# One shared product for levels 32 and 64 of a chunkwise gated recurrence, and shorter weight loads for levels 2 to 16

## Chip, cores and metric

The kernel runs on one core of one Trainium2 chip. The metric is device time in microseconds (us) of one execution. The five engines are named as in the profile: PE (TensorE: matmuls, with its weight loads shown apart as PEld), DVE (VectorE), ACT (ScalarE), POOL (GpSimd) and SP (SyncE, which issues the DMAs).

## The reference

A decoder trunk of two layers over 256 tokens and 1024 features, in float32: layer 0 is an HGRN2 gated linear recurrence, layer 1 a block-sparse attention; each is followed by a SwiGLU network, with RMS norms in between. The change touches the recurrence alone. Per head (8 heads, 128 state features, 128 value features):

```python
q = silu(q);  f = lb + (1 - lb) * sigmoid(fz);  k = 1 - f
S_t = diag(f_t) S_{t-1} + (1 - f_t) i_t^T
o_t = S_t^T q_t
```

Written without the state, `o_t` is the sum over `s <= t` of `score(t, s) * i_s`, where `score(t, s)` is the inner product, over the 128 features, of `q_t`, `k_s` and the product of all gates `f` from `s + 1` to `t`.

## The kernel before, in words

All weights are streamed once from DRAM in the order of their use, 1024 columns at a time ("sub"). Each sub is split into a high part `whi` (a copy on ACT, L412) and a low part `wlo` (a subtraction on DVE, L414), and each activation tile is split likewise, so that a float32 product is made of three fast products (`hi*hi`, `lo*hi`, `hi*lo`). `NSUB = 6` subs are held at a time. PE's main stream is these products: 128 x 128 weights with 256 tokens as the moving operand. `mm` at L455 issues every matmul, so all rows of PE carry that line and are told apart by their tiles.

The order of the work is planned when the program is built. The class `Order` keeps a clock for each engine and a list of waiting operations, each with an estimated cost (`ct`, `ca`, `cv` for PE, ACT and DVE) and a due time. The main products advance PE's clock; between them `pump` emits what is due and ready, and an operation of PE is emitted only once its inputs have been ready for 1500 ns of the plan (`EARLY`). Every engine then executes its own list strictly in order, with semaphores.

The recurrence of one head (class `Core`) runs beside the main products of the next one. After the projections of a head, `K[1]` holds the keys and `Q[1]` the queries, 128 features on the partitions and 256 tokens along the free axis (two chunks `a` of 128 tokens). `step(m)` makes level `2m` from level `m`: in each pair of neighbouring blocks of `m` places, the queries of the second block are multiplied by the gates of the first block's total, the keys of the first block by those of the second (DVE, L785 and L787), and the other halves are copied (ACT, L789 and L792). For `m = 64` the function `last` makes `q128` and `k128`, which join the two chunks (ACT, L800 to L803).

`scores` then multiplies, for each level m, the keys `K[m]` (as weights, 128 columns per chunk) with those queries that stand in the second block of a pair (64 columns per chunk, as the moving operand): function `level`, two matmuls per level. PE runs each of these plain float32 matmuls as two pairs of a weight load and a product. Level 1 has its own, wider product with `mov` (192 columns). Levels 2 and 4 share a PSUM bank, levels 8 and 16 another, and levels 32 and 64 a third (`b3`), which also takes the 128 x 128 product of `k128` and `q128`. Masked copies on DVE (`take`, L816) carry the entries of levels 1 to 16 that belong to the causal triangle into the score matrix `pm`; for the third bank the function `far` does it with four ACT copies of whole blocks (L853 to L856). `values` multiplies `pm` with the input tile `ii`, and `result` (L874 to L878) makes the output-gated, split tile `xh`, `xl` that the output projection `hgrn_w_out` reads. That projection takes heads 0 to 5 first, and heads 6 and 7 in its last 48 main products.

Of the kernel before, what the change touches and what calls it, by code (L numbers as in the profile page):

```python
# [12 lines left out]
AF = mybir.ActivationFunctionType  # L13
OP = mybir.AluOpType

P = 128
# [266 lines left out]
def cv(n, fast=False):  # L283
    return ((n / 2 if fast else n) + 66) / 0.96


def ca(n, ptr=0):
    return n / 1.2 + 93 + 93 * ptr
# [6 lines left out]
def ct(n):  # L295
    return 4 * max(n, P) / 2.4 + 3
# [6 lines left out]
def hybrid_trunk(ctx: ExitStack, tc: tile.TileContext, wts, xT, par, gfin, tab, onehot, masks, out):  # L303
    nc = tc.nc
    V, A, G, T = nc.vector, nc.scalar, nc.gpsimd, nc.tensor
# [5 lines left out]
    od = Order()  # L311
# [7 lines left out]
    def new(tag, shape, bufs=1, dt=FT, held=False):  # L319
        return ring(tag, shape, bufs, dt).new(held)  # L320
# [37 lines left out]
    def bank(g, held=False):  # L358
        return rings["ps" + g].new(held)
# [94 lines left out]
    def mm(o, a, b, start=False, stop=False):  # L454
        T.matmul(o, a, b, start=start, stop=stop, skip_group_check=True)  # L455
# [65 lines left out]
    for k0, k1 in [(k, k + 1) for k in range(4)] + [(4, 6), (6, 8)]:  # L521
        od.op("S", 60, lambda k0=k0, k1=k1: nc.sync.dma_start(hT[:, k0:k1, :], xT[:, k0:k1, :]),  # L522
              writes=hb[k0:k1], nbytes=131072 * (k1 - k0), due=8 * k0 - 6)
# [148 lines left out]
    for i in range(2):  # L672
        od.op("V", 80, lambda i=i: V.tensor_tensor(le[:, i], gain(5 + i), lbm.tile, op=OP.subtract), reads=[lbm],
              writes=[le], due=12)
# [5 lines left out]
          writes=[oml], due=30)  # L680
# [43 lines left out]
    class Core:  # L724
# [53 lines left out]
        def step(self, m, due):  # L778
            Q, K, tot = self.Q, self.K, self.tot[m]
            nb = S // (2 * m)  # L780
            if m < 64:
                q, qn, k, kn = Q[m], Q[2 * m], K[m], K[2 * m]
                v4 = lambda t: t.tile.rearrange("p (b z m) -> p b z m", z=2, m=m)
                bc = lambda z: tot.tile.rearrange("p (b z) -> p b z", z=2)[:, :, z:z + 1].to_broadcast([P, nb, m])
                od.op("V", cv(P), lambda: V.tensor_tensor(v4(qn)[:, :, 1], v4(q)[:, :, 1], bc(0), op=OP.mult),  # L785
                      reads=[q, tot], alloc=[qn], due=due)
                od.op("V", cv(P), lambda: V.tensor_tensor(v4(kn)[:, :, 0], v4(k)[:, :, 0], bc(1), op=OP.mult),  # L787
                      reads=[k, tot], alloc=[kn], due=due)
                o = od.op("A", ca(P), lambda: A.activation(v4(qn)[:, :, 0], v4(q)[:, :, 0], AF.Copy), reads=[q],  # L789
                          writes=[qn], due=due + .1)  # L790
                o.deps.append(qn.writers[0])
                o = od.op("A", ca(P), lambda: A.activation(v4(kn)[:, :, 1], v4(k)[:, :, 1], AF.Copy), reads=[k],  # L792
                          writes=[kn], due=due + .1)
                o.deps.append(kn.writers[0])
                return
            self.q128, self.k128 = q, k = new("q128", [P, P], 2), new("k128", [P, P], 2)
            Q, K = Q[64], K[64]

            def last():
                A.activation(q[:, 64:], Q[:, 192:], AF.Copy, scale=tot[:, 2:3])  # L800
                A.activation(q[:, :64], Q[:, P:192], AF.Copy)
                A.activation(k[:, :64], K[:, :64], AF.Copy, scale=tot[:, 1:2])
                A.activation(k[:, 64:], K[:, 64:P], AF.Copy)  # L803
            od.op("A", 4 * ca(64) + 186, last, reads=[Q, K, tot], alloc=[q, k], due=due)

        def scores(self, due):
            h, Q, K, mov = self.h, self.Q, self.K, self.mov
            pm = pms[h % 2]
            moff = {m: 2 * P + P * i for i, m in enumerate(LEVELS)}

            def take(b, c, m, stride=64):
                dst = pm.tile.rearrange("p a (b z m) -> p a b z m", z=2, m=m)
                src = b[:, c:c + 2 * stride].rearrange("p (a x) -> p a x", a=2)[:, :, stride - 64:]
                src = src.rearrange("p a (b m) -> p a b m", m=m)
                msk = mk[:, moff[m]:moff[m] + P].rearrange("p (a b m) -> p a b m", a=2, m=m)
                V.copy_predicated(dst[:, 0:3:2, :, 1], msk, src)  # L816

            def level(b, c, m):
                o = Q[m].tile.rearrange("p (a b z m) -> p a b z m", a=2, z=2, m=m)[:, :, :, 1]
                for a in range(2):  # L820
                    mm(b[:, c + 64 * a:c + 64 * a + 64], K[m][:, a * P:a * P + P], o[:, a], start=(c + a == 0), stop=True)

            b0 = bank("A")

            def s0():
                for a in range(2):
                    mm(b0[:, 192 * a:192 * a + 192], K[1][:, a * P:a * P + P], mov[:, a], start=(a == 0), stop=True)
            od.op("T", 2 * ct(192), s0, reads=[K[1], mov], alloc=[b0], due=due)

            def s0e():  # L830
                v = b0[:, :384].rearrange("p (a x) -> p a x", a=2)
                V.copy_predicated(pm[:, 0:3:2, :], mk[:, :2 * P].rearrange("p (a x) -> p a x", a=2), v[:, :, :P])
            od.op("V", cv(S), s0e, reads=[b0, mk], writes=[pm], due=due)
            od.op("V", cv(P), lambda: take(b0, 0, 1, 192), reads=[b0, mk], writes=[pm], due=due)
            for m in (2, 8):
                b = bank("A")
                o1 = od.op("T", 2 * ct(64), lambda b=b, m=m: level(b, 0, m), reads=[K[m], Q[m]], alloc=[b], due=due)
                o2 = od.op("T", 2 * ct(64), lambda b=b, m=m: level(b, P, 2 * m), reads=[K[2 * m], Q[2 * m]], writes=[b],
                           due=due)
                o2.deps.append(o1)  # L840
                for i in range(2):
                    od.op("V", cv(P), lambda b=b, m=m, i=i: take(b, P * i, m << i), reads=[b, mk], writes=[pm], due=due)
            b3 = bank("A")
            o1 = od.op("T", 2 * ct(64), lambda: level(b3, 0, 32), reads=[K[32], Q[32]], alloc=[b3], due=due)
            o2 = od.op("T", 2 * ct(64), lambda: level(b3, P, 64), reads=[K[64], Q[64]], writes=[b3], due=due)
            o3 = od.op("T", ct(P), lambda: mm(b3[:, 2 * P:3 * P], self.k128.tile, self.q128.tile, stop=True),
                       reads=[self.k128, self.q128], writes=[b3], due=due)
            o2.deps.append(o1)
            o3.deps.append(o2)

            def far():
                v = b3[:, :].rearrange("p (l a x) -> p l a x", l=4, a=2)
                A.activation(pm[0:32, 0:3:2, 32:64], v[0:32, 0, :, 0:32], AF.Copy)  # L853
                A.activation(pm[64:96, 0:3:2, 96:128], v[64:96, 0, :, 32:64], AF.Copy)
                A.activation(pm[0:64, 0:3:2, 64:128], v[0:64, 1], AF.Copy)
                A.activation(pm[:, 1, :], b3[:, 2 * P:3 * P], AF.Copy)  # L856
            od.op("A", 520, far, reads=[b3], writes=[pm], due=due)

            b4 = bank("A")
            hs = slice(h * P, h * P + P)  # L860

            def values():
                mm(b4[:, :S], ii[:, 0, hs], pm[:, 0:2, :].rearrange("p a t -> p (a t)"), start=True)
                mm(b4[:, P:S], ii[:, 1, hs], pm[:, 2, :], stop=True)
            od.op("T", ct(S) + ct(P), values, reads=[ii, pm], alloc=[b4], due=due)
            self.b4 = b4
# [14 lines left out]
    for h in range(NH):  # L881
        c = Core(h)
# [21 lines left out]
    for k in range(KT):  # L904
# [13 lines left out]
          reads=[tb], alloc=[tbr], due=80)  # L918
# [3 lines left out]
    for a in range(P // REP):  # L922
# [3 lines left out]
            reads=[scr_b], writes=[bt], nbytes=131072, due=90)  # L926
# [105 lines left out]
    def attend(h, qb, kb):  # L1032
# [20 lines left out]
        def scores():  # L1053
            mm(b[:, :P], q[:, :P], k[:, :P], start=True, stop=True)
            mm(b[:, P:384], qs[:, :P], kh.tile)
            mm(b[:, P:384], qs[:, P:], kh.tile)
            mm(b[:, P:384], qs[:, :P], kl.tile, stop=True)
        od.op("T", ct(P) + 3 * MM, scores, reads=[q, k, qs, kh, kl], alloc=[b], due=8)

        def logits():  # L1060
# [50 lines left out]
    for k in range(KT):  # L1111
# [8 lines left out]
          writes=[gf], due=100)  # L1120
# [152 lines left out]
```

## Time and profile before

| | us |
|---|---|
| median of 3 runs | 634.39 |
| the three runs | 634.28, 634.39, 639.41 |
| the profiled execution, own time | 636.15 |
| span of the profiled execution | 634.3 |
| PE busy in the span | 624.0 (98%) |
| ACT busy | 360.3 (57%) |
| DVE busy | 441.2 (70%) |

The span reaches from the first to the last instruction of the profiled execution; its own time is 1.85 us longer. The recurrence of the eight heads lies between 42 and 142 us of the span. Matmuls are pipelined, so the durations of neighbouring rows of PE overlap; what one costs is read from the distance between starts. The operations that one query of the timeline merges into a row carry their count (x8).

### The profile page before, as it was taken

Reading aid. Unit: us, or ns where it says so; the run is one execution under the profiler, and the core shown is the slowest. Engines: PE = TensorE matmul, PEld = TensorE weight load, DVE = VectorE, ACT = ScalarE, POOL = GpSimd, SP = SyncE. Lnnn points to the kernel's source line nnn. Section 1 sums busy time; section 2 is a strip of 40 time slices with the busy share of each in tenths; the row PEclk is TensorE's granted clock in tenths of the full one; section 3 lists DMA queues with packets and bytes.
Section 4 is the critical chain, followed back from the end, with each engine's and each line's share of the span. In section 5 each row is a group of like instructions: output and inputs, shape, how many; then the busy total and the mean of one; then the engine's idle time right before and its main releaser. Section 6 shows DMA issues by size and latency. Waiting matters only on the chain.

```text
span 634.3 us, 12520 instructions
## 1 busy us (share of the span) xinstructions
PE 624.0 (98%) x4900; PEld 600.9 (95%) x4900; DVE 441.2 (70%) x795; ACT 360.3 (57%) x691; POOL 38.8 (6%) x74
## 2 busy tenths in 40 slices
PE   8999999999999999999999999999999999999995
PEld 6899999999999999999998899999999999999994
DVE  6998787866786666666669578876685666666653
ACT  6798877755554444444446566655574444444442
POOL 0141112100400000000000000000100000000003
PEclk9999999999999999999999999999899999999998
DMA  8973434343796666665663664545556656666501
GB/s 284 329 230 130 137 100 140 129 137 131 204 256 193 197 196 195 198 194 189 190 197 118 215 207 159 167 135 198 167 165 199 198 188 187 183 184 184 175 1 67
DMA packets 32135, 111.83 MB, mean 176 GB/s; under 512 B 3835, under 2 KB 4508, under 8 KB 32076
## 3 DMA queue, kind: packets, MB, share of 16 engines
q1 hardware_dynamic: 31052, 108.71, 53.7%
q0 software_dynamic: 448, 1.25, 1.1%
q10 hardware_dynamic: 576, 1.08, 0.5%
q8 instruction: 38, 0.62, 0.4%
q14 instruction: 21, 0.17, 0.1%
HBM read 109.78 MB, written 1.25 MB: 175 GB/s over the span
## 4 chain that ended last, share of the span: by engine, by line
PE 95%; DMA 2%; ACT 1%; DVE 1%; SPq 0%; issue 0%; ACTq 0%
PE psA L455 47%; PE psB L455 47%; DMA raw<-in_w_dram 1%; DMA bt<-in_final_dram 1%; PE psB L1080 0%; ACT whi L412 0%; PE psB L1128 0%; SPq L401 0%; DVE sqacc L559 0%; SPq L522 0%; DVE wlo L414 0%; PE psA L596 0%; ACT xh L539 0%; DVE raw L1159 0%; ACT sq L1162 0%
## 5 line engine op out<-in xcount | busy, mean ns | idle before, releaser
L414 DVE TENSOR_TENSOR wlo<-raw,whi 128x1024 fp32r<-128x1024 f32 (+1 forms) x206 | 247.8, 1213 | 112.8 <-ACT whi L412 112.6
L412 ACT ACTIVATE whi<-raw 128x1024 fp32r<-128x1024 f32 (+1 forms) x205 | 213.1, 1050 | 153.2 <-issue 66.2
L455 PE MATMUL psB<-xh,whi 128*128 128x256 f32 x608 | 173.1, 288 | 0.0
L455 PE MATMUL psB<-xh,wlo 128*128 128x256 f32 x608 | 168.6, 280 | 0.0
L455 PE MATMUL psB<-xl,whi 128*128 128x256 f32 x608 | 163.0, 279 | 0.0
L455 PE MATMUL psA<-xh,whi 128*128 128x256 f32 x544 | 150.5, 280 | 0.0
L455 PE MATMUL psA<-xh,wlo 128*128 128x256 f32 x544 | 148.8, 277 | 0.0
L455 PE MATMUL psA<-xl,whi 128*128 128x256 f32 x544 | 143.7, 277 | 0.0
L455 PEld LDWEIGHTS psB<-xh,wlo 128*128 128x128 f32 x608 | 115.4, 190 | 0.7
L455 PEld LDWEIGHTS psB<-xh,whi 128*128 128x128 f32 x608 | 115.1, 189 | 0.8
L455 PEld LDWEIGHTS psB<-xl,whi 128*128 128x128 f32 x608 | 112.4, 190 | 0.0
L455 PEld LDWEIGHTS psA<-xh,whi 128*128 128x128 f32 x544 | 102.4, 188 | 0.6 <-issue 0.5
L455 PEld LDWEIGHTS psA<-xh,wlo 128*128 128x128 f32 x544 | 102.2, 188 | 0.0
L455 PEld LDWEIGHTS psA<-xl,whi 128*128 128x128 f32 x544 | 99.2, 188 | 0.0
L455 PE MATMUL psB<-hl,whi 128*128 128x256 f32 x176 | 48.7, 277 | 0.0
L455 PE MATMUL psB<-hh,whi 128*128 128x256 f32 x176 | 48.7, 277 | 0.0
L455 PE MATMUL psB<-hh,wlo 128*128 128x256 f32 x176 | 48.7, 277 | 0.0
L939 ACT ACTIVATE u<-sgq 128x256 f32<-128x256 f32 x44 | 18.0, 410 | 39.0 <-DVE sgq L937 38.7
L455 PE MATMUL psA<-wlo,hh 128*128 128x512 f32 x88 | 34.6, 393 | 0.0
L455 PE MATMUL psA<-whi,hl 128*128 128x512 f32 x88 | 34.5, 392 | 0.0
L455 PE MATMUL psA<-whi,hh 128*128 128x512 f32 x88 | 34.5, 392 | 0.0
L455 PEld LDWEIGHTS psB<-hl,whi 128*128 128x128 f32 x176 | 33.1, 188 | 0.0
(174 smaller groups left out, 795.5 us busy)
## 6 DMA issues: line engine op xcount, KB each, us to landing
raw<-in_w_dram SPq DMA_DIRECT2D x202, 512.0 KB, 4.2
raw<-in_w_dram SPq DMA_DIRECT2D x4, 256.0 KB, 4.1
bt<-scr POOLq DMA_DIRECT2D x8, 128.0 KB, 8.2
hT<-in_x_dram SPq DMA_DIRECT2D x4, 128.0 KB, 4.8
hT<-in_x_dram SPq DMA_DIRECT2D x2, 256.0 KB, 6.9
bt<-in_final_dram ACTq DMA_DIRECT2D x1, 512.0 KB, 5.1
out_dram<-raw ACTq DMA_DIRECT2D x2, 256.0 KB, 2.3
out_dram<-raw SPq DMA_DIRECT2D x2, 256.0 KB, 2.0
```

The source lines that it names most:

```text
L412: od.op("A", ca(n), lambda h=h, r=r, o=o, n=n: A.activation(h[:, :n], r[:, o:o + n], AF.Copy), reads=[r], alloc=[h], due=due)
L414: od.op("V", cv(n), lambda h=h, lo=lo, r=r, o=o, n=n: V.tensor_tensor(lo[:, :n], r[:, o:o + n], h[:, :n].bitcast(FT), op=OP.subtract), rea ...
L455: T.matmul(o, a, b, start=start, stop=stop, skip_group_check=True)
L939: od.op("A", ca(S), lambda: A.activation(sg.tile, gs.tile, AF.Sigmoid), reads=[gs], alloc=[sg], due=due)
```

## The change

In the last step before level 64 (`m == 32`), two ACT copies are added. The first writes places 96 to 127 of each chunk of `K[32]`, which hold keys that level 32 doesn't use, with the first 32 keys of level 64. The second writes the first blocks of `Q[32]` (places 0 to 31 and 64 to 95 of each chunk), which level 32 doesn't use either, with the 64 queries of level 64. One product per chunk over all 128 columns of `K[32]` and `Q[32]` then holds the scores of both levels, so the products of `K[64]` with `Q[64]` are gone. `far` picks the blocks out of the shared product with five ACT copies in place of four. For levels 2 to 16 only the first `128 - m` keys are loaded as weights, `take` reads `128 - m` partitions, and every product in these banks starts a fresh sum.

```diff
--- before.py
+++ after.py
@@ -792,6 +792,16 @@
                 o = od.op("A", ca(P), lambda: A.activation(v4(kn)[:, :, 1], v4(k)[:, :, 1], AF.Copy), reads=[k],
                           writes=[kn], due=due + .1)
                 o.deps.append(kn.writers[0])
+                if m == 32:
+
+
+                    v2 = lambda t: t.tile.rearrange("p (a x) -> p a x", a=2)
+                    od.op("A", ca(64), lambda: A.activation(v2(k)[:, :, 96:128], v2(kn)[:, :, 0:32], AF.Copy), reads=[kn],
+                          writes=[k], due=due + .2)
+                    od.op("A", ca(P), lambda: A.activation(
+                        q.tile.rearrange("p (a y z x) -> p a y z x", a=2, y=2, z=2)[:, :, :, 0],
+                        v2(qn)[:, :, 64:128].rearrange("p a (y x) -> p a y x", y=2), AF.Copy), reads=[qn], writes=[q],
+                        due=due + .2)
                 return
             self.q128, self.k128 = q, k = new("q128", [P, P], 2), new("k128", [P, P], 2)
             Q, K = Q[64], K[64]
@@ -813,12 +823,14 @@
                 src = b[:, c:c + 2 * stride].rearrange("p (a x) -> p a x", a=2)[:, :, stride - 64:]
                 src = src.rearrange("p a (b m) -> p a b m", m=m)
                 msk = mk[:, moff[m]:moff[m] + P].rearrange("p (a b m) -> p a b m", a=2, m=m)
-                V.copy_predicated(dst[:, 0:3:2, :, 1], msk, src)
+                r = P - m
+                V.copy_predicated(dst[:r, 0:3:2, :, 1], msk[:r], src[:r])
 
             def level(b, c, m):
+
                 o = Q[m].tile.rearrange("p (a b z m) -> p a b z m", a=2, z=2, m=m)[:, :, :, 1]
                 for a in range(2):
-                    mm(b[:, c + 64 * a:c + 64 * a + 64], K[m][:, a * P:a * P + P], o[:, a], start=(c + a == 0), stop=True)
+                    mm(b[:P - m, c + 64 * a:c + 64 * a + 64], K[m][:, a * P:a * P + P - m], o[:, a], start=True, stop=True)
 
             b0 = bank("A")
 
@@ -841,20 +853,26 @@
                 for i in range(2):
                     od.op("V", cv(P), lambda b=b, m=m, i=i: take(b, P * i, m << i), reads=[b, mk], writes=[pm], due=due)
             b3 = bank("A")
-            o1 = od.op("T", 2 * ct(64), lambda: level(b3, 0, 32), reads=[K[32], Q[32]], alloc=[b3], due=due)
-            o2 = od.op("T", 2 * ct(64), lambda: level(b3, P, 64), reads=[K[64], Q[64]], writes=[b3], due=due)
-            o3 = od.op("T", ct(P), lambda: mm(b3[:, 2 * P:3 * P], self.k128.tile, self.q128.tile, stop=True),
+
+            def both():
+                for a in range(2):
+                    c = slice(a * P, a * P + P)
+                    mm(b3[:, c], K[32][:, c], Q[32][:, c], start=True, stop=True)
+            o2 = od.op("T", 2 * ct(P), both, reads=[K[32], Q[32]], alloc=[b3], due=due)
+            o3 = od.op("T", ct(P), lambda: mm(b3[:, 2 * P:3 * P], self.k128.tile, self.q128.tile, start=True, stop=True),
                        reads=[self.k128, self.q128], writes=[b3], due=due)
-            o2.deps.append(o1)
             o3.deps.append(o2)
 
             def far():
-                v = b3[:, :].rearrange("p (l a x) -> p l a x", l=4, a=2)
-                A.activation(pm[0:32, 0:3:2, 32:64], v[0:32, 0, :, 0:32], AF.Copy)
-                A.activation(pm[64:96, 0:3:2, 96:128], v[64:96, 0, :, 32:64], AF.Copy)
-                A.activation(pm[0:64, 0:3:2, 64:128], v[0:64, 1], AF.Copy)
+                v = b3[:, :2 * P].rearrange("p (a x) -> p a x", a=2)
+                w = b3[:, :2 * P].rearrange("p (a y z x) -> p a y z x", a=2, y=2, z=2)[:, :, :, 0]
+                to = pm[:, 0:3:2, 64:128].rearrange("p a (y x) -> p a y x", y=2)
+                A.activation(pm[0:32, 0:3:2, 32:64], v[0:32, :, 32:64], AF.Copy)
+                A.activation(pm[64:96, 0:3:2, 96:128], v[64:96, :, 96:128], AF.Copy)
+                A.activation(to[32:64], w[32:64], AF.Copy)
+                A.activation(to[0:32], w[96:128], AF.Copy)
                 A.activation(pm[:, 1, :], b3[:, 2 * P:3 * P], AF.Copy)
-            od.op("A", 520, far, reads=[b3], writes=[pm], due=due)
+            od.op("A", 680, far, reads=[b3], writes=[pm], due=due)
 
             b4 = bank("A")
             hs = slice(h * P, h * P + P)
```

## Rows read from the trace of the kernel before

**Rows 1.** The page: busy us, share of the span, instructions of each engine.
```profile
PE 624.0 (98%) x4900; PEld 600.9 (95%) x4900; DVE 441.2 (70%) x795; ACT 360.3 (57%) x691; POOL 38.8 (6%) x74
```

**Rows 2.** The page: the chain that ended last, by engine.
```profile
PE 95%; DMA 2%; ACT 1%; DVE 1%; SPq 0%; issue 0%; ACTq 0%
```

**Rows 3.** Busy time in windows: stretch, length, engines, clock, DMA share, GB/s.
```profile
core 0: us, PE busy (x) PEld busy (x) DVE busy (x) ACT busy (x) POOL busy (x), PEclk, DMA share, GB/s
42.00:138.00 96.00, 96.00 (x810) 95.64 (x809) 76.87 (x197) 73.63 (x235) 17.39 (x42) 1.00 0.41 132
```

**Rows 4.** Timeline around 54 us: start us, us, engine, line, operation, out<-in.
```profile
54.13 0.98 PEld L455 LDWEIGHTS psA<-q,k 128*128 128x128 f32 x8
54.24 1.00 PE L455 MATMUL psA<-q,k 128*128 128x64 f32 x8
...
55.02 0.19 PEld L455 LDWEIGHTS psB<-xh,whi 128*128 128x128 f32 x1
55.05 0.36 PE L455 MATMUL psB<-xh,whi 128*128 128x256 f32 x1
...
55.25 0.28 PE L455 MATMUL psB<-xh,wlo 128*128 128x256 f32 x1
```

**Rows 5.** Timeline of PE around 62 us: the product of k128 and q128.
```profile
61.73 0.38 PE L455 MATMUL psA<-q,k 128*128 128x128 f32 x2
61.87 0.36 PE L455 MATMUL psB<-xh,whi 128*128 128x256 f32 x1
62.07 0.28 PE L455 MATMUL psB<-xh,wlo 128*128 128x256 f32 x1
```

**Rows 6.** Groups of PE by form: count | busy us, mean ns | idle before.
```profile
L455 PE MATMUL psA<-q,k 128*128 128x64 f32 x192 | 25.2, 264 | 0.0
```

**Rows 7.** Groups of ACT over the span: count | busy us, mean ns | idle before.
```profile
L789 ACT ACTIVATE q<-q 128x128 f32<-128x128 f32 x48 | 14.7, 306 | 1.3 <-DVE q L785 1.2
...
L855 ACT ACTIVATE pm<-psA 64x128 f32<-64x128 f32 x8 | 2.2, 272 | 0.1
...
L803 ACT ACTIVATE k<-k 128x64 f32<-128x64 f32 x8 | 1.9, 242 | 0.0
```

**Rows 8.** Timeline of ACT around 54 us: copies one behind the other.
```profile
54.36 0.26 ACT L856 ACTIVATE pm<-psA 128x128 f32<-128x128 f32 x1
54.52 0.30 ACT L789 ACTIVATE q<-q 128x128 f32<-128x128 f32 x1
54.72 0.30 ACT L792 ACTIVATE k<-k 128x128 f32<-128x128 f32 x1
```

**Rows 9.** Waits, 42 to 142 us: who waited for whom: us, times, longest.
```profile
ACT whi L412 <- PE psB L455: 2.7, 2, 1.9
```

**Rows 10.** The last head: timeline of DVE, then products by tile (first to last start).
```profile
142.42 0.42 DVE L878 TENSOR_TENSOR xl<-u,xh 128x256 fp32r<-128x256 f32 x1
...
L455 PE MATMUL psA<-xh,whi x14: 281/281/384, 154.8 to 159.7; 128*128 128x256 f32 x14
```

**Rows 11.** Timeline at 159 us: weights that fill 33 rows of the array.
```profile
158.88 0.29 PEld L455 LDWEIGHTS psB<-oh,tbr 33*128 33x128 f32 x2
158.88 0.91 PE L455 MATMUL psB<-oh,tbr 33*128 33x384 f32 x2
...
159.72 0.19 PEld L455 LDWEIGHTS psA<-xh,whi 128*128 128x128 f32 x1 [0.55 <-issue]
```

**Rows 12.** The chain in order of time: start us, us, what, products.
```profile
168.47 16.73 PE psA L455 x142
...
196.25 5.44 PE psA L455 x48
...
532.10 5.65 PE psB L455 x48
```

**Rows 13.** Timeline of PE at 447 us, then busy time in the window behind it.
```profile
447.10 1.02 PE L455 MATMUL psA<-ones,sqacc 128*128 128x1 f32 x8 [0.97 <-DVE sqacc L559]
...
449.00:453.00 4.00, 4.00 (x24) 4.00 (x23) 1.70 (x3) 0.76 (x3) 1.60 (x1) 0.57 0.81 233
```

## Prediction

> **What bounds the kernel now.** I read the page's shares first, then the chain, then windows over the stretch that the change touches. PE is busy for 98% of the span, DVE and ACT for 70% and 57% [rows 1]; the chain that ended last is PE for 95% [rows 2]. A share says nothing yet of this stage, so the window counts: from 42 to 138 us, where the recurrence of the heads runs beside the main products, PE is busy for 96.00 of 96.00 us, ACT for 73.63 and DVE for 76.87, at full granted clock [rows 3]. PE waits for nobody there. What leaves PE's list in this stretch comes off the end, unless another engine falls behind.
>
> What does a product of the recurrence cost PE? Its duration (264 ns) is no answer, since neighbours overlap; the distance between starts is. Eight products of 64 columns start at 54.24, the main product behind them at 55.05 and the next at 55.25 [rows 4]: 1.01 us for eight small products and one main one. A main product takes 0.118 us (142 of them in 16.73 us) [rows 12], so eight take 0.89 us, 0.112 each. Their loads say the same: eight from 54.13 to 55.02, 0.111 each. Now the product with 128 columns: two instructions and one main product from 61.73 to 62.07 [rows 5], 0.34 - 0.118 = 0.222, again 0.111 each. Twice the moving columns at the same price: in these products the weight load of 128 columns sets the pace, and the moving operand rides along.
>
> **The change, part by part.**
>
> *Levels 32 and 64 on PE.* There are 192 instructions of 64 columns [rows 6], which is 8 heads x 6 levels x 2 chunks x 2 passes. Levels 32 and 64 are 8 of them per head. In their place stand 2 chunks x 2 passes = 4 of 128 columns. By the two distances above, 8 x 0.112 = 0.89 us becomes 4 x 0.111 = 0.445 us: 0.446 us per head, 3.6 us over eight. No row has four of 128 columns in a line; were each to take as long as a main product (0.118), the saving would be 3.4 us. I take 3.6.
>
> *Shorter loads.* Levels 2, 4, 8 and 16 make 4 loads each per head, and leave out 2, 4, 8 and 16 of 128 columns. If a load's time goes with its columns, this is 4 x 0.112 x 30/128 = 0.105 us per head, 0.84 us in all; if a load costs 0.112 whatever it holds, nothing. Every load of the trace with all rows in use has 128 columns, so no row decides. I take 0.8: since the moving columns don't matter, the load is what is timed, and it is the load that shrinks; both ends stay in the range. Beside this stands the Trainium skill, "TensorE: Matmul & The Clock Gate", section "LDWEIGHTS (loading the stationary operand)": the time of a load is its number of columns divided by 1.2 GHz. By it this part would be an estimated 8 x 4 x 30/1.2 ns = 0.8 us and the whole 4.4 us; no run here shows a shorter load.
>
> *Fresh sums* (start on every product) change no count of instructions: nothing. *Masked copies* on 126 to 112 partitions have as many elements per partition as before: nothing, and DVE has 19 us to spare [rows 3].
>
> *ACT.* Added per head: a copy of 128x64 (as L803, 242 ns), one of 128x128 (as L789, 306 ns), and a fifth copy in `far`, where a 64x128 copy (272 ns) becomes two of 32x128 that I price alike [rows 7]. That is 0.82 us per head by duration, 6.6 us in all; by distance between starts, 0.16 and 0.20 us [rows 8], about 0.54 per head and 4.3 in all. ACT goes from 73.63 of 96 us to 78 to 80 of some 92: 85 to 87%. I cost it at nothing, because PE is hidden from ACT by the weights made in advance. ACT twice waits for PE to give a weight buffer back before it can make the next `whi` [rows 9]; then all six subs are full, and they are worth 6 x 8 x 3 products x 0.118 = 17 us of PE. Even 6.6 us of extra ACT work eats less than half. If that cover were gone, each microsecond of ACT would be one of PE, and the gain would turn into a loss of 2.2 us.
>
> *Waits.* The level-32 product used to need step 16 alone; the shared one needs step 32 and both fills, some 0.4 us of ACT behind it. On PE the next head's main products queue behind it, and the plan issues it 1.5 us after its inputs are due. I put that at nothing. `far` ends about 0.2 us later, and `values` and `result` behind it. For seven heads nobody on PE asks for that soon. For the last one, `xl` is done at 142.84 us [rows 10]. The first product of the next stage starts at 154.8 [rows 10], and heads 6 and 7 are read in the 48 products before it, so from 154.8 - 48 x 0.118 = 149.1 us. Of those 6.3 us the longer chain takes about 1 us, and a faster PE about another.
>
> *Sum.* 3.6 + 0.8 = 4.4 us. The profiled execution took 636.15 us, so it would take 631.75. The median of the runs is 634.39, 1.76 below the profiled one; taken from there, 630.0 us, a gain of 0.7%.
>
> **Rivals.**
>
> *1. The cadence of the main products moves.* This has nothing to do with the columns saved. The same main product comes every 0.118 us from 168 us on (16.73/142), every 0.113 from 196 on (5.44/48), and every 0.118 again from 532 on (5.65/48) [rows 12], with no change of loop at either turn. So PE has two cadences and stays in one until something disturbs it. Other groups of small products may leave it in the other. If the stretch from 188 to 338 us ran at 0.118 as well, it would cost 150 x (0.118/0.1133 - 1) = 6 us, and the kernel would end near 636. If the recurrence and its tail to 188 us, which are mostly slow now, became fast, it would gain up to 140 x 0.04 = 5 us at the very most; about 2 is nearer, since the fast cadence already shows up between groups. Then 628 or less. Likewise the granted clock averages 0.57 in the four microseconds from 449 us, mostly its lower level of 1.2 GHz, after PE had stood idle for 0.97 us and then run eight products of one column [rows 13]; that costs up to 4 x 0.43 = 1.7 us, which may come or go. Against a turn for the worse: the program behind 188 us is unchanged.
>
> *2. Short loads lose their overlap, and the kernel is slower.* Place: the 128 loads per run of levels 2 to 16. The one group with an array not full (33 rows) has no overlap: two products of 384 columns take from 158.88 to 159.72, and PEld stood idle for 0.55 us before its next load [rows 11]. At the pace of the 64-column products' own time (half of 0.112 each) behind a bare load, each of the 128 would take 0.056 us more, 7.2 us; at a full bare load each, 0.112, 14.3. With the 3.6 saved: 638 to 645. It decides as soon as a short load costs more than 3.6/128 = 0.028 us extra. Against it: that group lacks rows, not columns. The Trainium skill, "TensorEngine Tiling (Array Packing)", section "Key Properties", says that a change of tiling mode drains the engine; by its list of modes 112 columns and more are still the full-width mode, so by that rule this rival would not occur, while rows 11, with a smaller row mode, agree with a drain.
>
> *3. ACT takes the gain.* The fills make the shared product or `values` late, and PE waits at each head: 0.5 us a head is 4 us, and the kernel ends at 634. For it: ACT at 87% and strictly in order. Against it: rows 9 and the 1.5 us of the plan.
>
> *4. The load's length doesn't count.* Then 3.6 alone: 630.8.
>
> **How the numbers follow.** Forecast, with rival 4 in its reach: 0.6, 629 to 632. Rival 1, faster (626 to 628.5): 0.14; rival 1, slower (634 to 640): 0.09. Rival 2 (638 to 645): 0.07. Rival 3 (633 to 635): 0.10. The range runs from 626.5 to 636.0; it leaves out rival 2, half of slow rival 1 and a little at the low end, together under 0.2. About 1% is what a measurement tells from no change, so faster means below 628.05 and slower above 640.7. Of the fast side some 0.12 lies below 628.05, of rivals 1 and 2 some 0.05 above 640.7. The rest is 0.83.
>
> **What would show it.** In the profile after: 96 products of 128x64 gone (128 of them left, at 126 to 112 weights), 48 of 128x128 in place of 16, wait-free PE from 42 to 142 us, and a recurrence that ends some 4 us sooner. Groups of levels 2 to 16 shorter than 0.89 us per eight would show the loads right. Wrong would be: idle time of PE before `psA<-q,k` or `psA<-pm,ii` (rival 3), groups longer than 0.9 us (rival 2), or an unchanged program behind 190 us whose length has moved (rival 1).

## The result, and the profile after

The changed kernel takes 632.36 us (median of 18 runs, 631.48 to 633.65); the kernel before, run 18 times in all, 636.02 (634.28 to 639.41). The ratio is 0.9944, interval 0.9935 to 0.9953: 3.6 us faster, between 3.0 and 4.1. That is inside the range, and less than 1%, as forecast; the gain was forecast at 4.4 us. The profiled execution took 633.35 us, with a span of 631.6.

Shares and chain of the page hardly move. These two lines of the changed kernel answer to [rows 1, 2].

```profile
PE 621.1 (98%) x4868; PEld 597.7 (95%) x4868; DVE 440.2 (70%) x795; ACT 364.7 (58%) x715; POOL 36.4 (6%) x74
...
PE 94%; ACT 2%; DMA 2%; DVE 1%; issue 0%; SPq 0%; ACTq 0%
```

PE has 32 instructions less (4868 for 4900), four per head. ACT has 24 more, three per head, and its share of the chain is 2% where it was 1%. The window of the recurrence, to be held against [rows 3], shows both engines:

```profile
42.00:138.00 96.00, 95.52 (x807) 94.67 (x805) 76.39 (x195) 79.34 (x259) 14.94 (x42) 1.00 0.43 138
```

ACT is busy for 79.34 us where it was 73.63, as worked out (78 to 80). And PE is busy for 95.52 of 96.00: it waits now, which it didn't before. The waits of the changed kernel between 42 and 142 us (who waited for whom, us, times, longest) name the place; in the kernel before, no row of this list had PE in front.

```profile
PEld psA L455 <- ACT pm L874: 0.8, 1, 0.8
...
PE psA L455 <- ACT pm L874: 0.5, 1, 0.5
```

It is one wait, at one head. The timeline of the changed kernel around it:

```profile
119.78 0.61 PE L455 MATMUL psA<-q,k 128*128 128x128 f32 x4
...
120.25 1.99 ACT L412 ACTIVATE whi<-raw 128x1024 fp32r<-128x1024 f32 x2
...
121.99 0.38 PE L455 MATMUL psA<-q,k 128*128 128x128 f32 x2
...
122.62 0.92 PE L455 MATMUL psA<-mov,k 128*128 128x192 f32 x4
122.69 0.20 ACT L870 ACTIVATE pm<-psA 32x64 f32<-32x64 f32 x1
...
123.69 0.28 ACT L874 ACTIVATE pm<-psA 128x128 f32<-128x128 f32 x1
...
124.01 0.73 PEld L455 LDWEIGHTS psA<-pm,ii 128*128 128x128 f32 x4 [0.77 <-ACT pm L874]
...
124.77 0.55 PE L455 MATMUL psA<-q,k 128*126 128x64 f32 x4
```

Read it from the last row but one up. The weight loads of the product with the input tile stand idle for 0.77 us until L874, the last of the five copies of `far`, is through. The five take from 122.69 to 123.97, 1.28 us, where the plan counts 0.68; and they began 0.7 us after the start of the product of `q128` and `k128` at 121.99, because ACT had two `whi` conversions and two more copies in front of them.

What the wait costs is read from starts, against a head without it:

```profile
100.17 0.81 PE L455 MATMUL psA<-mov,k 128*128 128x192 f32 x4
100.81 0.82 PE L455 MATMUL psA<-pm,ii 128*128 128x256 f32 x4
...
101.59 0.28 PE L455 MATMUL psB<-xh,wlo 128*128 128x256 f32 x1
```

Here four products with `mov`, four with the input tile and one main product take 1.42 us, so the eight take 1.42 - 0.118 = 1.30. Around the wait the same eight take from 122.62 to 124.77, 2.15 us: 0.85 us more, within rounding the 0.84 that I use below.

The groups of small products show the two gains. First the group of level 16 (four products, 112 columns loaded), then the shared product (compare [rows 4, 5]); in each, the third row is the second main product behind the group, and 0.118 us of the distance to it belong to the first:

```profile
48.01 0.51 PE L455 MATMUL psA<-q,k 128*112 128x64 f32 x4
48.33 0.36 PE L455 MATMUL psB<-xh,whi 128*128 128x256 f32 x1
48.53 0.28 PE L455 MATMUL psB<-xh,wlo 128*128 128x256 f32 x1
...
50.18 0.61 PE L455 MATMUL psA<-q,k 128*128 128x128 f32 x4
50.55 0.36 PE L455 MATMUL psB<-xh,whi 128*128 128x256 f32 x1
50.75 0.28 PE L455 MATMUL psB<-xh,wlo 128*128 128x256 f32 x1
```

Four shared products and a main one take 0.57 us: (0.57 - 0.118)/4 = 0.113 each, the price forecast. Four of level 16 take (0.52 - 0.118)/4 = 0.1005 each, 0.011 less than with a full load.

Where does the rest of the run go? In the chain of the changed kernel (start, us, what), two pieces:

```profile
164.80 16.73 PE psA L455 x142
...
448.79 17.11 PE psB L455 x142
```

The first is the piece of [rows 12] that stood at 168.47, with the same length. The recurrence begins with the first product with `mov`, before and after at:

```profile
41.87 0.81 PE L455 MATMUL psA<-mov,k 128*128 128x192 f32 x4
```

```profile
41.53 0.81 PE L455 MATMUL psA<-mov,k 128*128 128x192 f32 x4
```

So from there to the piece it is 123.27 us where it was 126.60: 3.33 us gained. I use this length for all runs below. The second piece is 142 main products behind the last norm but one; in the chain of the kernel before, it was shorter:

```profile
452.21 16.46 PE psB L455 x142
```

Here 0.65 us is given back, in a part of the program that the change doesn't touch.

### The profile page after: what moved, and what is told of

Its sections match the earlier page's. It is cut to its first block, busy times and chain, and to the rows that moved or that the text cites. A ratio compares the mean times of both kernels' runs of the same rounds, so it can differ in the third digit from the quotient of the medians.

```text
span 631.6 us, 12483 instructions
## 1 busy us (share of the span) xinstructions
PE 621.1 (98%) x4868; PEld 597.7 (95%) x4868; DVE 440.2 (70%) x795; ACT 364.7 (58%) x715; POOL 36.4 (6%) x74
## 4 chain that ended last, share of the span: by engine, by line
PE 94%; ACT 2%; DMA 2%; DVE 1%; issue 0%; SPq 0%; ACTq 0%
PE psB L455 47%; PE psA L455 47%; DMA bt<-in_final_dram 1%; DMA raw<-in_w_dram 1%; ACT whi L412 1%; PE psB L1098 0%; PE psB L1146 0%; DVE sqacc L559 0%; PE psA L596 0%; ACT xh L539 0%; ACT k L792 0%; DVE raw L1177 0%; ACT sq L1180 0%; ACT raw L1207 0%; DVE wlo L414 0%
```

## The experiments

All are timed against the kernel before on the same chip. "Length" is that of the recurrence as above. My theory: the gain is the sum of products (3.6 us) and loads (0.64 us, from the groups of the profile after), less one wait of 0.84 us, which comes from ACT's order at one head. Rivals: ACT holds PE back throughout; shorter loads are hidden, or lose their overlap; the cadence of the main products (the distance between the starts of two neighbours) decides.

| kernel | ratio to before | interval | length, us |
|---|---|---|---|
| before | 1 | | 126.60 |
| the change | 0.9944 | 0.9935 to 0.9953 | 123.27 |
| the change again | 0.9943 | 0.9929 to 0.9957 | 123.28 |
| shared product only | 0.9952 | 0.9940 to 0.9964 | 124.17 |
| short loads only | 0.9996 | 0.9987 to 1.0005 | 126.04 |
| product issued later | 0.9930 | 0.9917 to 0.9942 | 122.47 |
| copies planned at their price | 0.9931 | 0.9916 to 0.9945 | 122.38 |
| fills on POOL | 0.9939 | 0.9923 to 0.9955 | 122.39 |
| fills on POOL, product later | 0.9933 | 0.9918 to 0.9947 | 122.24 |
| fills twice | 0.9947 | 0.9931 to 0.9964 | 123.10 |
| 96 keys loaded | 0.9920 | 0.9906 to 0.9935 | 121.93 |
| 72 keys loaded | 0.9896 | 0.9879 to 0.9913 | 120.12 |
| 64 keys loaded | 0.9996 | 0.9983 to 1.0009 | 126.08 |

### The two parts apart

The shared product alone has full loads again:

```diff
-                r = P - m
+                r = P
...
-                    mm(b[:P - m, c + 64 * a:c + 64 * a + 64], K[m][:, a * P:a * P + P - m], o[:, a], start=True, stop=True)
+                    mm(b[:, c + 64 * a:c + 64 * a + 64], K[m][:, a * P:a * P + P], o[:, a], start=True, stop=True)
```

> The changed kernel with all 128 keys loaded again at levels 2 to 16; the order of the instructions on PE is that of the changed kernel. If the parts add up (my theory): the four-product groups of levels 4, 8 and 16 go back from 0.55, 0.54 and 0.52 us (with the main product behind them) to 0.565, the run loses 8 x 0.08 = 0.64 us against the changed kernel and stays some 3 us under the kernel before (ratio 0.995). If the shorter loads are hidden (rival: the length of a load doesn't count in the end): the same time as the changed kernel, ratio 0.9944. The wait of PE near 124 us should stay in both.

Measured: ratio 0.9952, and a length of 124.17 us, 0.90 more than the change. Its group of level 16, in the timeline of PE:

```profile
48.23 0.55 PE L455 MATMUL psA<-q,k 128*128 128x64 f32 x4
...
48.79 0.28 PE L455 MATMUL psB<-xh,wlo 128*128 128x256 f32 x1
```

0.56 us in place of 0.52, at otherwise the same order of PE. The wait near 124 us is there too. So the loads are not hidden. The ratio alone could not tell 0.9952 from 0.9944, since the intervals overlap; the groups and the length can.

The length moved by 0.90 and not 0.64, and the starts of PE say why. Between two neighbouring main products it is either 0.113 or 0.118 us. In the recurrence of the change I count 238 of the one and 431 of the other, here 164 and 505: 74 x 0.0045 = 0.3 us that has nothing to do with the loads. The distances at the small products add up to 0.6.

The loads alone, in the kernel before (levels 32 and 64 keep full loads):

```diff
+                r = P - m
-                V.copy_predicated(dst[:, 0:3:2, :, 1], msk, src)
+                V.copy_predicated(dst[:r, 0:3:2, :, 1], msk[:r], src[:r])
...
+                    r = P - m if m < 32 else P
-                    mm(b[:, c + 64 * a:c + 64 * a + 64], K[m][:, a * P:a * P + P], o[:, a], start=(c + a == 0), stop=True)
+                    mm(b[:r, c + 64 * a:c + 64 * a + 64], K[m][:, a * P:a * P + r], o[:, a], start=True, stop=True)
...
```

> The kernel before with the shorter loads of levels 2 to 16 alone; levels 32 and 64 keep their own products. If the parts add up: 0.64 us faster than before, ratio 0.999, within reach of the cadence of the main products (up to 1 us either way). If the shorter loads cost their overlap somewhere (rival): slower than before. No wait of PE for ACT, since nothing is added on ACT.

Measured: 0.9996, which can't be told from no change, and a length of 126.04 us, 0.56 less than before: the size expected, and no wait of PE. The rival of slower loads falls at these widths, by the length; the ratio doesn't tell.

### The wait near 124 us

One number of the plan, the lead of the product with the input tile:

```diff
-            od.op("T", ct(S) + ct(P), values, reads=[ii, pm], alloc=[b4], due=due)
+            od.op("T", ct(S) + ct(P), values, reads=[ii, pm], alloc=[b4], due=due, early=2500.0)
```

> The changed kernel with one number of the plan changed: the product of the scores with the inputs is issued on PE 2.5 us after its scores are due, not 1.5. If the changed kernel loses 0.84 us at one place, because five ACT copies take 1.28 us where the plan has 0.68 (my theory): the wait of PE near 124 us goes, and the run is 0.8 us faster than the changed kernel, ratio 0.993. If ACT holds PE back throughout (rival): the wait moves to another head, and the time stays.

Measured: 0.9930, a length of 122.47, 0.80 less than the change. PE is busy throughout again, with ACT at least as busy as in the change:

```profile
42.00:138.00 96.00, 96.00 (x812) 95.58 (x812) 77.55 (x198) 80.11 (x265) 17.78 (x42) 1.00 0.40 136
```

No wait has PE in front, at this head or another. The next run leaves the lead alone and gives the plan the real price of the five copies:

```diff
-            od.op("A", 680, far, reads=[b3], writes=[pm], due=due)
+            od.op("A", 1280, far, reads=[b3], writes=[pm], due=due)
```

> The changed kernel with the plan's cost of the five copies of the shared product set to 1280 ns, which is what they took at the late place, in place of 680. If the wait near 124 us comes from the plan's price being 0.6 us too low (my theory): the wait goes, and the time is that of the kernel whose products of the scores are issued later, ratio 0.993. If it comes from the order of ACT at that head whatever the price (rival): a wait of 0.2 to 0.8 us remains, ratio 0.994.

Measured: 0.9931, 122.38 us, and no wait of PE:

```profile
42.00:138.00 96.00, 96.00 (x813) 95.58 (x812) 78.22 (x199) 80.15 (x262) 14.70 (x42) 1.00 0.43 139
```

Either number of the plan removes the wait; both runs reorder the other engines too, so what is shown is that a plan with more room for `far` has no wait, and that ACT's amount of work doesn't force one.

The fills on POOL take that work off ACT:

```diff
-                    od.op("A", ca(64), lambda: A.activation(v2(k)[:, :, 96:128], v2(kn)[:, :, 0:32], AF.Copy), reads=[kn],
+                    od.op("G", cg(64), lambda: G.tensor_copy(v2(k)[:, :, 96:128], v2(kn)[:, :, 0:32]), reads=[kn],
...
-                    od.op("A", ca(P), lambda: A.activation(
+                    od.op("G", cg(P), lambda: G.tensor_copy(
...
```

> The changed kernel with both fills done by POOL in place of ACT. ACT gets back 8 x 0.55 = 4.4 us of busy time, POOL has 15 us busy of 96. If ACT's load costs only the one wait of 0.84 us (my theory): 0 to 0.8 us faster than the changed kernel. If ACT holds PE back throughout (rival): faster by 2 us or more. If POOL's copies are slow (the multiplications of 128 elements on it take 0.9 us) and lengthen the chain behind the shared product: a new wait of PE, and up to 1 us slower.

Measured: 0.9939 and 122.39 us. The window:

```profile
42.00:138.00 96.00, 96.00 (x812) 95.58 (x812) 78.29 (x199) 77.58 (x246) 23.33 (x58) 1.00 0.40 139
```

ACT falls from 79.34 to 77.58 only, and PE's wait is gone; the gain in length is 0.88, that of the wait and no more. The rival asked for 2 us or more.

> Both mendings together: the fills on POOL, and the products of the scores issued 2.5 us after their inputs are due. Either alone showed no wait of PE any more. If that wait was all that ACT cost (my theory): nothing is added to either, ratio 0.993, within 0.0012. If ACT's load still costs something that shows up in no wait of PE (rival): 0.992 or less.

Both mendings together (the diffs are those above): 0.9933 and 122.24 us. Nothing is added. The opposite test gives ACT more:

```diff
+                    for _ in range(2):
...
```

(the two fills stand in the loop)

> The changed kernel with both fills done twice over, the second time without effect on the result. ACT gets 4.4 us more to do beside the recurrence. If ACT's work is hidden by weights made 12 to 19 us ahead (my theory): the time of the changed kernel, but for single waits of some tenths where five copies come late, 1 us at the most. If ACT is what takes the gain (rival): 4 us slower than the changed kernel, and no faster than before.

Measured: 0.9947 and 123.10 us, with ACT at 82.15 us of 96 in the same window and a single wait of PE's loads of 0.7 us:

```profile
42.00:138.00 96.00, 95.62 (x808) 94.87 (x807) 76.59 (x197) 82.15 (x277) 15.70 (x42) 1.00 0.41 139
```

Three amounts of ACT work, 77.6, 79.3 and 82.2 us, and the length follows none of them; it follows the one wait. The rival falls.

### How far a load can shrink

The same edit with 96, 72 and 64 in place of `P - m`. These kernels leave out the other keys of levels 2 to 16, so they measure what a load costs and are no replacement. Here 96:

```diff
-                r = P - m
+                r = 96
...
-                    mm(b[:P - m, c + 64 * a:c + 64 * a + 64], K[m][:, a * P:a * P + P - m], o[:, a], start=True, stop=True)
+                    mm(b[:96, c + 64 * a:c + 64 * a + 64], K[m][:, a * P:a * P + 96], o[:, a], start=True, stop=True)
```

> The changed kernel with 96 keys loaded at each of the levels 2 to 16; keys 96 to 127 of each chunk are left out of these levels. Order of PE as in the changed kernel. If a load shrinks by the 0.66 ns per column that levels 8 and 16 show (my theory): 32 columns less are 0.021 us, a product comes every 0.091 us, and the run is 128 x 0.021 - 0.64 = 2 us faster than the changed kernel. If it goes with its whole 0.112 us (0.875 ns per column): every 0.084 us, 2.9 us faster. If a load that isn't full loses its overlap (rival 2): slower.

The timeline of PE, a group of four and the second main product behind it:

```profile
47.76 0.47 PE L455 MATMUL psA<-q,k 128*96 128x64 f32 x4
...
48.25 0.28 PE L455 MATMUL psB<-xh,wlo 128*128 128x256 f32 x1
```

(0.49 - 0.118)/4 = 0.093 us a product, as expected from 0.66 ns per column. In length only 1.34 us is gained of 2: PE is now early enough to meet two more short waits (0.2 us each, for copies of ACT at L789 and L766), and 492 of its distances between main products are 0.118 us where the change has 431, 0.3 us more.

> The changed kernel with 64 keys loaded at each of the levels 2 to 16; keys 64 to 127 of each chunk are left out of these levels. If the time of a load goes on shrinking by 0.66 ns per column: a product every 0.070 us, 128 x 0.042 - 0.64 = 4.7 us faster than the changed kernel; 64 moving columns alone take 0.055. If a load of half the array's width is a change of its mode and drains it (rival 2 at this width): a product every 0.112 us or more and no gain over the changed kernel, or a loss.

The second of the two came. The timeline with 64 keys; mark where the load begins:

```profile
48.13 0.28 PE L455 MATMUL psB<-xl,whi 128*128 128x256 f32 x1
...
48.33 0.31 PEld L455 LDWEIGHTS psA<-q,k 128*64 128x64 f32 x4
48.33 0.45 PE L455 MATMUL psA<-q,k 128*64 128x64 f32 x4
...
48.93 0.28 PE L455 MATMUL psB<-xh,wlo 128*128 128x256 f32 x1
```

0.60 us: 0.120 a product on average, more than with a full load, and the length is 126.08, 2.8 us above the change. Was it the width of 64, or does the overlap fade as loads get shorter?

> The changed kernel with 72 keys loaded at each of the levels 2 to 16; keys 72 to 127 of each chunk are left out of these levels. Order of PE as in the changed kernel. With 96 keys a product came every 0.092 us, with 64 keys every 0.120. If the width of 64 columns is what costs the overlap (my theory), 72 keys go on the line of 96: 0.092 - 24 x 0.0007 = 0.075 us a product, groups of four with the main product behind them at 0.42 us, and some 2 us faster than with 96. If the overlap fades as loads get shorter (rival): 0.10 to 0.12 us a product, slower than with 96.

The timeline with 72 keys:

```profile
47.80 0.28 PE L455 MATMUL psB<-xl,whi 128*128 128x256 f32 x1
47.80 0.39 PEld L455 LDWEIGHTS psA<-q,k 128*72 128x72 f32 x4
...
47.92 0.41 PE L455 MATMUL psA<-q,k 128*72 128x64 f32 x4
...
48.34 0.28 PE L455 MATMUL psB<-xh,wlo 128*128 128x256 f32 x1
```

0.42 us: (0.42 - 0.118)/4 = 0.0755 a product, and a length of 120.12, 1.8 us less than with 96, with further short waits of PE for ACT. The first load starts at 47.80, with the main product in front of the group, and so lies beside it. With 64 keys it starts at 48.33, 0.20 behind the start of that main product (48.13) and together with its own product. So the overlap does not fade: at 72 columns it is there, and at 64 the first load of a group has lost it.

Are all loads of 64 columns dear, or only the first? Where two levels stand side by side, eight products follow each other. First 64 keys, then 72, each with the second main product behind:

```profile
81.42 0.68 PE L455 MATMUL psA<-q,k 128*64 128x64 f32 x8
...
82.25 0.28 PE L455 MATMUL psB<-xh,wlo 128*128 128x256 f32 x1
```

```profile
78.81 0.67 PE L455 MATMUL psA<-q,k 128*72 128x64 f32 x8
...
79.50 0.28 PE L455 MATMUL psB<-xh,wlo 128*128 128x256 f32 x1
```

With 64 keys eight take 0.83 us and four 0.60, so four more cost 0.23, 0.058 each: less than the 0.068 with 72 keys ((0.69 - 0.42)/4). Inside a group the short load pays. What is lost is lost where PE changes between 128 and 64 columns: some 0.08 us in front of the group (0.20 for 0.12), and 0.60 - 0.118 - 4 x 0.058 = 0.25 from its first product on, where the same sum gives 0.03 with 72 keys.

The groups also tell the price of a column. With all 128 columns, four products take 0.56 and eight 1.01 us ([rows 4]), with 72 they take 0.42 and 0.69. If the first load of a group saves nothing, because it lies beside the main product in front, three loads of four and seven of eight count: 0.14/(3 x 56) = 0.83 and 0.32/(7 x 56) = 0.82 ns per column. The two agree; shared out over all four and all eight loads they would be 0.63 and 0.71.

### The change again

> The changed kernel once more, unaltered. If its main products from 450 to 468 us keep the slow cadence (0.118 us) by the program, this profile has it again and the span is 631.6 us within 0.3; if the cadence there is left to chance (my theory, from timed runs between 631.5 and 633.7), another profile shows the fast one (0.113) and is up to 0.9 us shorter. The wait of PE near 124 us should come back, within 0.2 us of 0.84.

Measured: 0.9943, and the length 123.28, equal to the first profile within 0.01 us; the wait of 0.8 us is there again. The cadence came again too: the 142 products behind the norm take 16.73 us, 0.118 each. With the product with the input tile issued later they take 16.11, 0.113. From the chains of the two:

```profile
447.92 16.73 PE psB L455 x142
```

```profile
449.07 16.11 PE psB L455 x142
```

So my theory that chance sets it is not borne out: two profiles of one program have the same cadence. What differed was the clock, in the same window of the repeated profile and of the first:

```profile
447.00:450.00 3.00, 2.52 (x22) 2.52 (x23) 0.69 (x1) 2.05 (x3) 0.43 (x1) 1.00 0.88 251
```

```profile
447.00:450.00 3.00, 3.00 (x18) 3.00 (x17) 0.31 (x1) 1.18 (x2) 0.86 (x1) 0.58 0.89 277
```

In the repeated profile the clock was granted in full (1.00, 2.4 GHz) where in the first it averaged 0.58, mostly its lower level of 1.2 GHz. In front of it PE had stood idle, waiting for the sums of squares (L559), and had then run products of one column. First in the repeated profile, then in the first:

```profile
443.28 1.02 PE L455 MATMUL psA<-ones,sqacc 128*128 128x1 f32 x8 [0.59 <-DVE sqacc L559]
```

```profile
443.71 1.02 PE L455 MATMUL psA<-ones,sqacc 128*128 128x1 f32 x8 [1.27 <-DVE sqacc L559]
```

In two executions of one program the clock fell behind 1.27 us of idling and not behind 0.59. It also fell behind the 0.97 of [rows 13]; but with 96 keys loaded, behind the same 0.97 us at the same place, it did not:

```profile
441.96 1.02 PE L455 MATMUL psA<-ones,sqacc 128*128 128x1 f32 x8 [0.97 <-DVE sqacc L559]
```

```profile
445.00:448.00 3.00, 2.45 (x22) 2.25 (x21) 0.56 (x2) 1.37 (x3) 1.11 (x1) 1.00 0.83 246
```

So the length of the idling in front does not settle it alone. The span of the repeated profile is 630.3 us, 1.3 shorter. A single profile can so carry more than 1 us that comes and goes, through the clock and the idling in front of it. Timed runs of the changed kernel spread by 2.2 us; what part of that is the clock is not shown.

The second cadence has a consequence for the table. The profiles of the four kernels without the wait all show 0.113 behind the norm, and both of the change show 0.118: 0.6 us of what divides their ratios has nothing to do with the wait. The length leaves that piece out.

## Why the prediction was right, and where it was off

*What bounds the kernel:* right. In the recurrence, every run in which PE lost products became shorter by about their price; what it gave back were waits of PE and the cadence of the main products.

*Levels 32 and 64, 3.6 us:* right. Four shared products cost 0.113 us each, as the two distances said; the change less its loads and with its wait taken out gives 126.60 - 124.17 + 0.84 = 3.3 us of length, and the groups alone 3.6. Of the 0.3 between them the cadence takes most: 505 distances of 0.118 us where the kernel before has 451, 54 x 0.0045 = 0.24 us. One count was wrong beside the sum: among its signs the prediction names 96 products of 64 columns gone, and it is 64 (192 to 128), the 8 per head that the sum itself used.

*Shorter loads, 0.8 us:* the term that was mis-sized; the groups give 0.6. The reading that a load's time goes with its columns was right, and so was the price, 0.83 ns per column against the 0.112/128 = 0.875 of the sum. The step that failed is the count of the loads: all four of a level were taken to shrink in PE's time, but the first of a group lies beside the main product in front and saves nothing. Three loads of four are 8 x 3 x 30 x 0.83 ns = 0.6 us. The Trainium skill, "TensorE: Matmul & The Clock Gate", section "LDWEIGHTS (loading the stationary operand)", divides the columns by 1.2 GHz, 0.83 ns each; these runs agree, with 0.83 and 0.82, for the loads behind the first. The kernel with short loads alone gained 0.56 us of length.

*ACT and the waits, nothing:* the step that failed. The cover by weights made in advance held: with ACT busy for 5.7 us more, PE has no wait for `whi` in the recurrence. But I had looked only at how far ahead the weights are, and not at the product that waits for `far` itself. I put the waits of the chain at nothing because of the plan's lead of 1.5 us; the plan counted five copies at 0.68 us that take 1.28, and queued two conversions of 1 us in front of them at one head. That is rival 3 at one head in eight, 0.84 us in place of 4. The room at the other heads is small: with PE faster still (96 and 72 keys) further waits for ACT appear.

*Rival 1:* its mechanism exists, and it took 0.65 us in a place I hadn't named, behind the recurrence at 449 us. From 165 to 182 us, where I feared a change, the piece has the same 16.73 us in every run.

*Rival 2:* wrong for 126 to 112 columns, right for 64. By the Trainium skill, "TensorEngine Tiling (Array Packing)", section "Key Properties", a change of tiling mode drains the engine, and the list of modes there has one of 64 columns. These runs agree: with 64 keys the time is lost at the change (0.20 us in front of the group for 0.12 with 72 keys, and 0.25 from its first product on for 0.03) and not between two products of 64 columns (0.058 us each).

*The number itself:* 630.0 for 632.4. Some 0.8 us is the gain, and 1.6 us the starting point: three runs had a median of 634.39, eighteen have 636.02. Against the profiled executions (636.15 and 633.35) the gain is 2.8 us for 4.4: 0.2 too much for the loads, 0.84 of the wait and 0.65 of the cadence behind the recurrence make 1.7. The range was wide enough for both errors; neither the cadence behind the norm nor the 1.6 us between the medians is a term of the sum.

## What to carry to other kernels

Where the distance between small products is the same for 64 and 128 moving columns, the load is what is paid: fill the moving operand, or share a load, before anything else. Cut the weight columns as far as the data allow; the first load of each group saves nothing, since it lies beside the product in front. 72 columns still paid. A few products of 64 columns between products of 128 did not, because the change between the two costs more than they save. And when work is added to an engine that isn't the bound, check not only its cover in the large (weights made ahead) but every product that waits for exactly that work, with the measured price of the work in the plan: here a price 0.6 us too low went with a wait of 0.8 us, and one number of the plan won it back (a length of 122.47 for 123.27). The ratios, 0.9930 for 0.9944, can't be used for that: their intervals overlap, and the cadence behind the norm moved as well. The four kernels without the wait can't be told apart by their times.

## What was not expected of the hardware

A group of four products with loads of 64 columns, half of the array, costs more than one with 128: 0.120 us a product against 0.1105, while 72 columns cost 0.0755. It is the change from 128 columns to 64 and back that costs; between themselves the products of 64 columns come every 0.058 us. And the main products have two cadences, 0.113 and 0.118 us. The 142 products from the end of the recurrence on took 16.73 us in every run; the 142 behind the norm came every 0.113 us in eight of the thirteen profiles and every 0.118 in five. The repeated program kept its cadence. What sets it stays open.
